# A hybrid decoder trunk on one core: index queries cut to 192 columns, and a list scheduler with new costs and rules

## The chip, the cores and the metric

One core of one Trainium2 chip runs the whole program. The metric is the device time of one execution in microseconds (us). The engines are TensorE (PE in the profile, its weight loads PEld), VectorE (DVE), ScalarE (ACT), GpSimd (POOL) and the queue that issues transfers (SP).

## What is computed

Two layers over 256 tokens of width 2048. In each layer a normed x goes through one large input projection, whose columns feed three branches (a chunked state-space scan, A; a delta-rule recurrence, B; sparse attention with a token indexer, C) and their merge gates; then a branch projection, gated sum, output projection, norm and residual. The part that the change touches directly is the indexer of branch C:

```python
top_k = min(TOPK_MAX, S // 4)                 # 64 of 256 keys
logits_idx = jnp.einsum('bqhd,bsd->bqhs', iqb, ik)
score = jnp.einsum('bqh,bqhs->bqs', iwb, jax.nn.relu(logits_idx))
score = jnp.where(causal[None], score, -jnp.inf)
_, sel = lax.top_k(score, top_k)
valid = sel <= qpos[None, :, None]
```

A query at position below 64 has at most 64 causal keys, so it gets all of them whatever its scores are.

## The kernel before

All projections are products of 128x128 weight blocks with 256 tokens, in float32r with each operand split in a high and a low part: `acc` issues three matmuls for one product of blocks (high by high, high by low, low by high). `block` (L702) runs one block of 128 output columns over the 16 row blocks of the input, so 48 matmuls of 256 columns; `unit` (L713) runs two such blocks into one PSUM tile of the tag `psg` (3 banks). The halves of the weights come by DMA as `wraw`, ScalarE rounds them to `whi`, VectorE subtracts to make `wlo`. The normed input is `hh` (high) and `hl` (low).

`proj_c` (L1264) has the units of branch C: keys, values, then four units of index queries (two heads in each block; 128 columns of weights by 256 tokens), then queries and gates. After each index unit `rope` (L793) makes `iq` from PSUM with four elementwise operations of 128x512: a product on VectorE, a shuffle on VectorE, a product and a sum on GpSimd. `index_scores` (L1186) then makes the scores of each head and `select` (L1207) the mask.

The work of the branches beside the projections uses plain float32 matmuls into PSUM tiles of the tag `psa` (5 banks). A float32 product appears in the trace as two passes, so as two MATMUL records. Most have 128 rows and 128 columns of weights. In `rwkv_chunk` (L1097) there are products of 64x64 weights by 64 columns: the step `pA` has four of them (`UT` with `X`, tile names `ut` and `t`), in a group of two heads whose `X[0]` and two whose `X[1]` was made by another operation; it runs four times for each of eight groups of four heads in the two layers together, 32 times. The step `pB` (`NM` with `SA`, names `b_nm` and `zp`) also has four and runs 16 times.

The order of the instructions on each engine is not that of the program text. `note` (L255) records every operation with its dependencies, its rank (lower goes first) and its cost in ns by the table in `cost` (L289); `issue` (L315) then plays the whole kernel through in a list schedule: when an engine is free at the model's time t it takes, of the recorded operations with all predecessors scheduled, the first by rank and program order whose operands are ready by the model and whose tile has a buffer. A result counts as ready after the operation's end plus a latency: `LP` 200 ns for TensorE, `LD` 140 for VectorE and ScalarE, `PO` 300 for GpSimd, and `LT` 130 more where TensorE is the reader. The order found is what the engines run; on the chip each engine goes through its list in order and waits where an operand is late. The lines of `cost` that the prediction speaks of:

```python
if r[0].dtype in (F32R, BF):
    return n / 2.4 + 1.7, 0.0
if op == "transpose":
    return n / 1.2, 0.0
return n / 0.6 * (0.4 if ... else 0.58 if out.shape[0] <= 64 else 1.05), 0.0
```

Every instruction carries the line of the scheduler's last loop, L418, so groups in the profile are told apart by tile names.

Of the kernel before, what the change touches and what calls it, by code (L numbers as in the profile page):

```python
# [11 lines left out]
F32R = mybir.dt.float32r  # L12
BF = mybir.dt.bfloat16
# [6 lines left out]
DM, S, NL = 2048, 256, 2  # L20
NK = DM // 128
OA, OB, OC, OG = 0, 3088, 7312, 10976
NEG = -1.0e30
GONE = -3.0e38
KAP = 0.5 * math.exp(-0.5)
N1, N2 = 43, 9
WB = 4
# [4 lines left out]
PG = 3  # L32
# [158 lines left out]
    return {"x": x, "post": post, "pos": pos, "par": par, "w2a2": w2a2, "wst": wst, "cst": consts()}  # L191


LP = 200
LD = 140
LT = 130
PT = 180
PO = 300
LW = 0.83
SQ = [(9,), (1, 3)]  # L200

# [1 line left out]
class Program:  # L203
# [51 lines left out]
    def note(self, eng, op, f, a, k):  # L255
        w = [k["out"] if "out" in k else a[0]] + [k[n] for n in ("accum_out",) if n in k]
        r = [x for x in list(a[("out" not in k):]) + [v for n, v in k.items() if n not in ("out", "accum_out")]
             if isinstance(x, bass.AP)]
        i = len(self.ops)
        deps = set()  # L260
        tiles = set()
        for aps, writes in ((r, False), (w, True)):
            for ap in aps:
                g = self.region(ap)
                if g[0] in self.tiles:
                    tiles.add(g[0])
                elif ap.space == bass.MemoryType.DRAM and not g[0].startswith(("diag", "out")):
                    continue
                ws, rs = self.seen.setdefault(g[0], ({}, {}))
                hit = lambda q: q[0] < g[2] and g[1] < q[1] and q[2] < g[4] and g[3] < q[3]  # L270
                deps.update(j for q, j in ws.items() if hit(q))
                if writes or ap.space == bass.MemoryType.PSUM:

                    deps.update(j for j, q in rs.items() if hit(q) and (writes or self.ops[j][0] != eng))
                    inside = lambda q: g[1] <= q[0] and q[1] <= g[2] and g[3] <= q[2] and q[3] <= g[4]
                    for q in [q for q in ws if inside(q)]:
                        del ws[q]
                    for j in [j for j, q in rs.items() if inside(q)]:
                        del rs[j]
                    ws[g[1:]] = i  # L280
                else:
                    rs[i] = g[1:]
        deps.discard(i)
        for t in tiles:
            self.tiles[t][2] += 1
        self.ops.append((eng, op, f, a, k, deps, tiles, self.rank, self.cost(eng, op, w[0], r, k), w[0].shape[0]))

    @staticmethod
    def cost(eng, op, out, r, k):  # L289

        n = int(np.prod(out.shape[1:]))
        if op == "dma_start":
            b = 4.0 * n * out.shape[0]
            return {"SP": 500.0, "ACT": 500.0, "POOL": 1050.0}[eng], b
        if eng == "PE":
            if r[0].dtype in (F32R, BF):
                return n / 2.4 + 1.7, 0.0
            if op == "transpose":
                return n / 1.2, 0.0
            return n / 0.6 * (0.4 if r[0].shape[0] <= 32 or out.shape[0] <= 32 else 0.58 if out.shape[0] <= 64 else 1.05), 0.0  # L300
        m = max([n] + [int(np.prod(x.shape[1:])) for x in r])
        ps = any(x.space == bass.MemoryType.PSUM for x in r)
        sc = sum(int(np.prod(x.shape[1:])) == 1 for x in r) if m > 1 else 0
        if eng == "ACT":
            return (51.0 if ps else 94.0) + 0.833 * m + 93.0 * min(sc, 2) + (46.0 if "accum_out" in k else 0.0), 0.0
        if eng == "DVE":
            fast = op in ("tensor_scalar", "tensor_copy") and not ps
            return 70.0 + (0.52 if fast else 1.042) * m + 61.0 * (sc > 0), 0.0
        if op in ("memset", "affine_select"):
            return 35.0 + (0.83 if op == "memset" else 1.27) * m, 0.0  # L310
        if op == "tensor_scalar":
            return 374.0 * m / 256 + 83.0 * sc, 0.0
        return PT + 2.1 * m, 0.0

    def issue(self, tc):  # L315
        ops = self.ops
# [3 lines left out]
        ready = [0.0] * N  # L320
# [3 lines left out]
                users[j].append(i)  # L324
        cand = {e: [] for e in self.ENGINES}
        add = lambda i: insort(cand[ops[i][0]], (ops[i][7], i))
        for i in range(N):
            if not left[i]:
                add(i)
# [4 lines left out]
        names = {tag: names for tag, (_, names) in self.tags.items()}  # L334
        used = {tag: 0 for tag in self.tags}
        clk = {e: 0.0 for e in self.ENGINES}
        dma = 0.0
        table = 0
        last = 200.0
# [6 lines left out]
        while len(order) < N:  # L346
            t, k, e = heappop(events)
            best = None
            later = None
            until = None  # L350
            for c in cand[e]:
                i = c[1]
                if i > front + AHEAD or until and t + ops[i][8][0] > until:
                    continue
                if ready[i] > t:
                    if c[0] < 0 and ready[i] < t + 250.0 and not until:
                        until = ready[i]
                    later = ready[i] if later is None else min(later, ready[i])
                    continue
                ok = True  # L360
                for n in ops[i][6]:
                    if first[n]:
                        tag, no = self.tiles[n][:2]
                        al, dd = alive[tag], dead[tag]
                        while dd and dd[0][0] <= t:
                            al.remove(heappop(dd)[1])
                        held = used[tag] - (len(names[tag]) - len(al))
                        room = self.tags[tag][0]
                        if held >= room or held >= room - KEEP.get(tag, room) and bisect_left(al, no) >= room:
                            ok = False  # L370
                            break
                if ok:
                    best = c
                    break
# [5 lines left out]
            idle = 0  # L380
            cand[e].remove(best)
            i = best[1]
            _, op, f, a, kw, deps, tiles, _, (busy, b), _ = ops[i]
            order.append(i)
            while front < N and end[front] is not None:
                front += 1
# [1 line left out]
                table = self.TABLES[a[2]]  # L388
                busy += 1300.0
            if e == "PE":  # L390
                w = ops[i][9]
                busy += max(0.0, LW * w - last)
                last = ops[i][8][0]
            clk[e] = t + busy
            if op == "dma_start":
                dma = max(dma, t + busy + 650.0) + b / 360.0
# [3 lines left out]
            for n in tiles:  # L400
                used[self.tiles[n][0]] += first[n]
                first[n] = False
                q = self.tiles[n]
# [4 lines left out]
            for j in users[i]:  # L408
                left[j] -= 1
                to = ops[j][0]  # L410
                ready[j] = max(ready[j], t + busy if to == e == "PE" else end[i] + (LT if to == "PE" else 0.0))
                if not left[j]:
                    add(j)
            heappush(events, (clk[e], k, e))
# [24 lines left out]
class Trunk:  # L439
# [259 lines left out]
        self.mm(out, w[0], x[1], False, False)  # L699
        self.mm(out, w[1], x[0], False, last)  # L700

    def block(self, l, out, x, nch):  # L702

        n = 8 * nch
        for k in range(n):
            if k % 4 == 0:
                w = self.half()
            self.acc(out, [None if q is None else q[:, 128 * (k % 4):128 * (k % 4) + 128] for q in w],
                     [None if q is None else q[k] if isinstance(q, list) else q[:, k, :] for q in x], k == 0, k == n - 1)
            if k % 4 == 3:  # L710
                self.pump()

    def unit(self, l, x, n=2, nch=2):  # L713
        p = self.P("g", PG).rearrange("p (b t) -> p b t", b=2)
        for i in range(n):
            self.block(l, p[:, i, :], x, nch)
        return p

    def split(self, src, hi, lo, scale=None):
# [70 lines left out]
    SWAP = [(i + 16) % 32 for i in range(32)]  # L790

    @urgent
    def rope(self, outs, x, n):  # L793

        P = x.shape[0]
        bc = lambda a: a[:P].to_broadcast([P, n, S])
        t = self.t2(2, S)[:P, :n]
        u = self.t2(2, S)[:P, :n]
        self.v.tensor_tensor(t, x, bc(self.cos), op=OP.mult)
        self.v.stream_shuffle(u, x, self.SWAP)  # L800
        self.g.tensor_tensor(u, u, bc(self.sin), op=OP.mult)
        for o in outs:
            self.g.tensor_tensor(o, t, u, op=OP.add)
# [403 lines left out]
    def select(self):  # L1207
# [6 lines left out]
        for sl in (slice(128, 384), slice(0, 128)):  # L1214
            for _ in range(8):
                yield
                v.max(m8, sc[:, sl])
                v.match_replace(sc[:, sl], m8, sc[:, sl], GONE)
        v.tensor_scalar(sc, sc, 0.9 * GONE, NEG, op0=OP.is_gt, op1=OP.mult)
        kb = self.T([128, 384], "c_kb", 1, BF)  # L1220
# [43 lines left out]
    def proj_c(self, l, h):  # L1264
        s = self.s
        p = self.unit(l, h)
# [8 lines left out]
        for k in range(16):  # L1275
            if k % 2 == 0:
                w = self.half()
# [8 lines left out]
        self.score = self.t2(384)  # L1286
        self.kb = None
        for n in range(4):
            p = self.unit(l, h)
            iq = self.t2(2, S)  # L1290
            self.rope([iq], p, 2)
            self.spawn("C", self.index_scores(iq, n))
            yield
        self.spawn("C", self.select())
        self.yc = self.T([128, 8, S], "yc")
        for n in range(4):
            p = self.unit(l, h)
            if n == 0:
                self.q = self.T([128, 8, S], "ya")
            q = self.q[:, 2 * n:2 * n + 2, :]  # L1300
            self.rope([q], p, 2)
            yield
            p = self.unit(l, h)
# [262 lines left out]
```

## Time and profile before

| | |
|---|---|
| median of 3 runs | 2396.93 us (2394.79 to 2397.88) |
| the profiled execution | 2396.85 us |
| its span, first to last instruction | 2395.1 us |
| PE busy | 2357.6 us, 98% |
| DVE, ACT, POOL busy | 1645.2, 1302.5, 514.3 us |
| mean granted TensorE clock | 0.994 of full speed |

The span and the 1.75 us around it make the execution's own time. A matmul's bar in the trace is longer than its share of the engine, since matmuls are pipelined; what a matmul costs is the distance from its start to the next start.

### The profile page before, as it was taken

The numbers are of one execution on the slowest core, as the hardware profiler recorded it, in microseconds if no ns is written. First come the engines' busy times: TensorE is split into PE (matmuls) and PEld (weight loads), VectorE is DVE, ScalarE is ACT, GpSimd is POOL, SyncE is SP. The second block draws the span as 40 slices with busy tenths as digits, with TensorE's granted clock in tenths as the row PEclk, the third lists the DMA queues.
The fourth block names the chain that finished last, engine by engine and source line by source line (L and its number), as shares of the span: only waits on it lengthen the run. The fifth ranks groups of instructions, "written<-read, shape, count | busy, mean of one in ns | idle before, by whom it ended". The sixth has DMA issues, their size and how long they took to land.

```text
span 2395.1 us, 49317 instructions
## 1 busy us (share of the span) xinstructions
PE 2357.6 (98%) x18750; PEld 2277.0 (95%) x18750; DVE 1645.2 (69%) x3466; ACT 1302.5 (54%) x2674; POOL 514.3 (21%) x915
## 2 busy tenths in 40 slices
PE   8999999999999999999989999999999999999998
PEld 7999999999999999998889999999999999999987
DVE  8865967778795555556576769676787855555565
ACT  5755565656554554445456555656555545545453
POOL 2252252414110000101112513433150100101001
PEclk9999999999999999999999999999999999999999
DMA  5444443535445665656544534434354556656563
GB/s 194 145 159 126 147 152 104 160 108 170 153 150 187 205 225 191 203 187 216 174 143 145 165 118 147 140 119 147 110 188 137 166 186 215 217 187 199 188 214 129
DMA packets 149583, 396.09 MB, mean 165 GB/s; under 512 B 47905, under 2 KB 51937, under 8 KB 149089
## 3 DMA queue, kind: packets, MB, share of 16 engines
q1 hardware_dynamic: 149344, 392.94, 50.4%
q8 instruction: 147, 2.41, 0.4%
q14 instruction: 92, 0.75, 0.1%
HBM read 386.55 MB, written 6.32 MB: 164 GB/s over the span
## 4 chain that ended last, share of the span: by engine, by line
PE 93%; DVE 4%; issue 1%; ACT 1%; DMA 1%; SPq 0%; DVEq 0%; ACTq 0%
PE psg L418 78%; PE psa L418 15%; DVE t L418 2%; DVE wlo L418 1%; DVE yb L418 0%; ACT t L418 0%; DVE ya L418 0%; DMA wraw<-in_wst 0%; DVE n_x L418 0%; ACT whi L418 0%; DMA vd<-diag 0%; DMA yb<-in_x 0%; DVE c_mx L418 0%; SPq L418 0%; DVE yc L418 0%
## 5 line engine op out<-in xcount | busy, mean ns | idle before, releaser
L418 DVE TENSOR_TENSOR wlo<-wraw,whi 128x512 fp32r<-128x512 f32 x1352 | 978.1, 725 | 620.2 <-ACT whi L418 612.9
L418 ACT ACTIVATE whi<-wraw 128x512 fp32r<-128x512 f32 x1361 | 858.2, 632 | 895.9 <-PE psg L418 811.0
L418 PE MATMUL psg<-hh,whi 128*128 128x256 f32 x4224 | 1210.2, 287 | 0.0
L418 PE MATMUL psg<-hl,whi 128*128 128x256 f32 x4224 | 1194.9, 283 | 1.0 <-DVE hl L418 1.0
L418 PE MATMUL psg<-hh,wlo 128*128 128x256 f32 x4224 | 1193.7, 283 | 0.0
L418 PEld LDWEIGHTS psg<-hl,whi 128*128 128x128 f32 x4224 | 796.7, 189 | 6.2 <-DVE hl L418 1.3
L418 PEld LDWEIGHTS psg<-hh,whi 128*128 128x128 f32 x4224 | 796.7, 189 | 5.6 <-issue 1.2
L418 PEld LDWEIGHTS psg<-hh,wlo 128*128 128x128 f32 x4224 | 796.2, 188 | 3.2
L418 PE MATMUL psg<-t,whi 128*128 128x256 f32 x1536 | 274.1, 280 | 0.0
L418 PEld LDWEIGHTS psg<-t,whi 128*128 128x128 f32 x1536 | 234.1, 188 | 0.2
L418 PE MATMUL psg<-t,wlo 128*128 128x256 f32 x768 | 214.8, 280 | 0.0
L418 POOL TENSOR_TENSOR t<-t,t 128x256 f32<-128x256 f32 (+25 forms) x298 | 157.0, 528 | 261.5 <-DVE t L418 179.4
L418 POOL TENSOR_TENSOR b_nm<-b_nm,t 128x256 f32<-128x256 f32 x64 | 47.9, 748 | 737.8 <-DVE t L418 714.8
L418 PEld LDWEIGHTS psg<-t,wlo 128*128 128x128 f32 x768 | 144.3, 188 | 0.1
L418 POOL TENSOR_TENSOR t<-t,d 128x60 f32<-128x60 f32 (+24 forms) x248 | 104.4, 421 | 83.0 <-DMA d<-diag 43.8
L418 ACT ACTIVATE t<-psa 128x256 f32<-128x256 f32 (+5 forms) x230 | 93.4, 426 | 45.4 <-PE psa L418 44.4
L418 PE MATMUL psg<-whi,hh 128*128 128x512 f32 (+1 forms) x268 | 98.8, 369 | 0.0
L418 PE MATMUL psg<-wlo,hh 128*128 128x512 f32 (+1 forms) x268 | 97.8, 365 | 0.0
L418 PE MATMUL psg<-whi,hl 128*128 128x512 f32 (+1 forms) x268 | 97.0, 364 | 0.0
L418 PE MATMUL psa<-t,zp 128*128 128x128 f32 (+1 forms) x448 | 82.5, 299 | 1.1 <-ACT t L418 0.7
L418 PE MATMUL psa<-t,zl 128*128 128x256 f32 x256 | 67.5, 385 | 3.3 <-DVE t L418 2.3
L418 PEld LDWEIGHTS psa<-t,zp 128*128 128x128 f32 x448 | 65.9, 191 | 4.3 <-ACT t L418 1.1
(244 smaller groups left out, 2369.1 us busy)
## 6 DMA issues: line engine op xcount, KB each, us to landing
wraw<-in_wst SPq DMA_DIRECT2D x688, 512.0 KB, 3.4
d<-diag SPq DMA_DIRECT2D x32, 128.0 KB, 3.9
t<-diag SPq DMA_DIRECT2D x16, 256.0 KB, 3.9
d<-in_wst SPq DMA_DIRECT2D x8, 512.0 KB, 5.2
ya<-in_x SPq DMA_DIRECT2D x8, 256.0 KB, 4.3
yb<-in_x SPq DMA_DIRECT2D x8, 256.0 KB, 5.2
b_nm<-in_post SPq DMA_DIRECT2D x2, 1024.0 KB, 6.9
out_x<-ya SPq DMA_DIRECT2D x8, 256.0 KB, 2.8
```

Of the source, the lines that this page charges most:

```text
L418: ops[i][2](*ops[i][3], **ops[i][4])
```

## The change

It cuts the index queries to tokens 64 to 255 and writes zeros for the rest; it replaces costs and one latency of the scheduler; it adds to the model a charge for a change of matmul form and for VectorE and GpSimd running at the same time; and it holds the first matmul of each group of consecutive `psa` matmuls that write one bank. The core of the diff:

```diff
+TOP = 64
+SLACK = 300
+SWITCH = 90
-PT = 180
-PO = 300
+PO = 200
@@ note
+        form = None
+        size = lambda x: int(np.prod(x.shape[1:]))
+        sb = [x for x in r if x.space != bass.MemoryType.PSUM and size(x) > 1]
+        if eng == "PE":
+            cut = lambda n: 32 if n <= 32 else 64 if n <= 64 else 128
+            form = cut(r[0].shape[0]), cut(size(r[0]))
+        elif eng == "DVE":
+            form = size(w[0]) >= 8 and (len(sb) > 1 or len(sb) == len([x for x in r if size(x) > 1])
+                                        and op in ("tensor_scalar", "tensor_copy"))
+        elif eng == "POOL":
+            form = op != "memset"
@@ cost
-                return n / 2.4 + 1.7, 0.0
+                return n * 0.442 + 5.0 if r[0].shape[0] > 64 else n / 1.2, 0.0
             if op == "transpose":
-                return n / 1.2, 0.0
-            return n / 0.6 * (0.4 if ... else 0.58 if out.shape[0] <= 64 else 1.05), 0.0
+                return 30.0, 0.0
+            return 2 * max(n / 1.2 + 2.0, LW * int(np.prod(r[0].shape[1:]))), 0.0
...
-        return PT + 2.1 * m, 0.0
+        return (170.0 if m > 200 else 110.0) + 2.05 * m, 0.0
@@ issue
+        batch = {}
+        run = None
+        for i, o in enumerate(ops):
+            bank = o[0] == "PE" and o[3][0].tensor.name
+            if bank and bank.startswith("psa"):
+                if run is None or run[3] != bank or i - 1 not in batch:
+                    run = [i, 0, 0.0, bank]
+                batch[i] = run
+                run[1] += sum(batch.get(j) is not run for j in o[5])
...
+                late = ready[i]
+                if e == "PE" and i in batch:
+                    if i == batch[i][0]:
+                        if ops[i][10] != (128, 128):
+                            if batch[i][1]:
+                                continue
+                            late = batch[i][2]
+                        if c[0] > 0:
+                            late += SLACK
+                if late > t:
...
             if e == "PE":
-                w = ops[i][9]
-                busy += max(0.0, LW * w - last)
-                last = ops[i][8][0]
+                busy += SWITCH if form != cut else max(0.0, LW * ops[i][9] - last)
+                cut = form
+                last = ops[i][8][0] / (1 if ops[i][3][1].dtype in (F32R, BF) or op == "transpose" else 2)
+            elif form:
+                busy += max(0.0, port["POOL" if e == "DVE" else "DVE"] - t - 55.0)
+                port[e] = t + busy
@@ proj_c, with the slice ts passed on through unit, block and rope
-            p = self.unit(l, h)
+            ts = slice(TOP, S)
+            p = self.unit(l, h, ts=ts)
             iq = self.t2(2, S)
-            self.rope([iq], p, 2)
+            self.g.memset(iq[:, :, 0:TOP], 0.0)
+            self.rope([iq[:, :, ts]], p, 2, ts)
```

`batch[i][1]` counts the operands of the group that are not yet scheduled, `batch[i][2]` is the model's time when the last of them is ready. For a group whose weights are not of the form 128x128 the first matmul is held until all operands of the group are there; for every group of rank over 0 it is held `SLACK` ns longer. ScalarE's costs are also changed by some tens of ns.

## Rows read from the trace of the kernel before

**Rows 1.** The page: busy us and share of the span, instructions.

```profile
PE 2357.6 (98%) x18750; PEld 2277.0 (95%) x18750; DVE 1645.2 (69%) x3466; ACT 1302.5 (54%) x2674; POOL 514.3 (21%) x915
```

**Rows 2.** The page: the chain that ended last, by engine.

```profile
PE 93%; DVE 4%; issue 1%; ACT 1%; DMA 1%; SPq 0%; DVEq 0%; ACTq 0%
```

**Rows 3.** Stretches: us, busy (instructions) of PE, PEld, DVE, ACT, POOL; granted clock, DMA.

```profile
500.00:600.00 100.00, 98.58 (x798) 96.36 (x798) 86.68 (x213) 61.25 (x138) 36.75 (x74) 1.00 0.49 160
...
700.00:1100.00 400.00, 400.00 (x3428) 399.89 (x3428) 232.01 (x372) 202.05 (x352) 27.39 (x42) 1.00 0.60 197
```

**Rows 4.** Timeline of PE around one run of eight 64x64 passes: start us, bar us.

```profile
365.14 0.28 PE L418 MATMUL psg<-hh,whi 128*128 128x256 f32 x1
365.35 0.68 PE L418 MATMUL psa<-zp,b_nm 64*64 64x64 f32 x8
365.95 0.39 PE L418 MATMUL psg<-hl,whi 128*128 128x256 f32 x1
366.18 0.28 PE L418 MATMUL psg<-hh,wlo 128*128 128x256 f32 x1
```

**Rows 5.** Timeline of PE around one run of four 64x64 passes.

```profile
634.05 0.28 PE L418 MATMUL psg<-hh,wlo 128*128 128x256 f32 x1
634.25 0.44 PE L418 MATMUL psa<-t,ut 64*64 64x64 f32 x4
634.63 0.38 PE L418 MATMUL psg<-hh,whi 128*128 128x256 f32 x1
634.85 0.28 PE L418 MATMUL psg<-hl,whi 128*128 128x256 f32 x1
```

**Rows 6.** Groups of PE by form, whole span: count, busy us, mean ns.

```profile
L418 PE MATMUL psa<-t,ut 64*64 64x64 f32 x256 | 28.2, 230 | 0.0
...
L418 PE MATMUL psa<-zp,b_nm 64*64 64x64 f32 x128 | 10.8, 224 | 0.0
```

**Rows 7.** Timeline of PE in the output projection, 512 columns.

```profile
1118.97 0.40 PE L418 MATMUL psg<-whi,hl 128*128 128x512 f32 x1
...
1120.13 0.40 PE L418 MATMUL psg<-wlo,hh 128*128 128x512 f32 x1
```

**Rows 8.** Timeline of PE's weight loads right after a transpose, and in a row of eight.

```profile
300.08 0.19 PEld L418 LDWEIGHTS psg<-hh,whi 128*128 128x128 f32 x1
300.19 0.19 PEld L418 LDWEIGHTS psg<-hl,whi 128*128 128x128 f32 x1
...
211.29 0.86 PEld L418 LDWEIGHTS psa<-cst,vd 128*128 128x128 f32 x8
```

**Rows 9.** A product of `rope` on POOL (whole span) and a small zeroing there.

```profile
L418 POOL TENSOR_TENSOR t<-t,sin 128x512 f32<-128x512 f32 x18 | 29.5, 1636 | 114.9 <-DVE t L418 114.9
...
L418 POOL MEMSET b_cu<- 128x2 f32 x2 | 0.2, 102 | 0.0
```

**Rows 10.** PE's waits, 100 to 1100 us (last: 1260 to 2300): total us, times, longest.

```profile
PE psa L418 <- DVE t L418: 4.3, 7, 1.2
PE psa L418 <- ACT t L418: 0.7, 2, 0.3
PE psa L418 <- POOL t L418: 0.5, 1, 0.5
PE psa L418 <- ACT zl L418: 0.5, 1, 0.5
...
PE psa L418 <- DVE t L418: 4.2, 7, 1.2
```

**Rows 11.** Timeline of PE around one such wait.

```profile
596.13 0.28 PE L418 MATMUL psg<-hh,whi 128*128 128x256 f32 x1
597.30 0.33 PE L418 MATMUL psa<-cst,t 128*128 128x128 f32 x1 [0.90 <-DVE t L418]
```

**Rows 12.** POOL products of 128x256 from 100 to 700 us; VectorE's weight split there.

```profile
L418 POOL TENSOR_TENSOR t<-t,t 128x256 f32<-128x256 f32 x14 | 12.2, 868 | 57.2 <-DVE t L418 38.1 <-DVE c_sm L418 18.0 <-ACT t L418 0.9
...
L418 DVE TENSOR_TENSOR wlo<-wraw,whi 128x512 fp32r<-128x512 f32 x297 | 216.2, 729 | 106.6 <-ACT whi L418 104.3 <-issue 0.5 <-PE psg L418 0.2
```

More of the change, by code (lines that the diff above doesn't have):

```diff
@@ L285, in note @@
             self.tiles[t][2] += 1
-        self.ops.append((eng, op, f, a, k, deps, tiles, self.rank, self.cost(eng, op, w[0], r, k), w[0].shape[0]))
+        form = None
[9 more added lines that the diff above has]
+            form = op != "memset"
+        self.ops.append((eng, op, f, a, k, deps, tiles, self.rank, self.cost(eng, op, w[0], r, k), w[0].shape[0], form))
     @staticmethod
@@ L296, in cost @@
             if r[0].dtype in (F32R, BF):
-                return n / 2.4 + 1.7, 0.0
+                return n * 0.442 + 5.0 if r[0].shape[0] > 64 else n / 1.2, 0.0
             if op == "transpose":
-                return n / 1.2, 0.0
-            return n / 0.6 * (0.4 if r[0].shape[0] <= 32 or out.shape[0] <= 32 else 0.58 if out.shape[0] <= 64 else 1.05), 0.0
+                return 30.0, 0.0
+            return 2 * max(n / 1.2 + 2.0, LW * int(np.prod(r[0].shape[1:]))), 0.0
         m = max([n] + [int(np.prod(x.shape[1:])) for x in r])
@@ L304, in cost @@
         if eng == "ACT":
-            return (51.0 if ps else 94.0) + 0.833 * m + 93.0 * min(sc, 2) + (46.0 if "accum_out" in k else 0.0), 0.0
+            return (51.0 if ps else 105.0) + 0.836 * m + 93.0 * min(sc, 2) + (95.0 if "accum_out" in k else 0.0), 0.0
         if eng == "DVE":
@@ L309, in cost @@
         if op in ("memset", "affine_select"):
-            return 35.0 + (0.83 if op == "memset" else 1.27) * m, 0.0
+            return 35.0 + (0.83 if op == "memset" else 1.32) * m, 0.0
         if op == "tensor_scalar":
             return 374.0 * m / 256 + 83.0 * sc, 0.0
-        return PT + 2.1 * m, 0.0
+        return (170.0 if m > 200 else 110.0) + 2.05 * m, 0.0
     def issue(self, tc):
@@ L336, in issue @@
         clk = {e: 0.0 for e in self.ENGINES}
+        port = {"DVE": 0.0, "POOL": 0.0}
+        cut = None
         dma = 0.0
@@ L354, in issue @@
                     continue
-                if ready[i] > t:
+                late = ready[i]
[8 more added lines that the diff above has]
+                if late > t:
                     if c[0] < 0 and ready[i] < t + 250.0 and not until:
                         until = ready[i]
-                    later = ready[i] if later is None else min(later, ready[i])
+                    later = late if later is None else min(later, late)
                     continue
@@ L382, in issue @@
             i = best[1]
-            _, op, f, a, kw, deps, tiles, _, (busy, b), _ = ops[i]
+            _, op, f, a, kw, deps, tiles, _, (busy, b), _, form = ops[i]
             order.append(i)
@@ L411, in issue @@
                 ready[j] = max(ready[j], t + busy if to == e == "PE" else end[i] + (LT if to == "PE" else 0.0))
+                if j in batch and batch.get(i) is not batch[j]:
+                    batch[j][1] -= 1
+                    batch[j][2] = max(batch[j][2], ready[j])
                 if not left[j]:
@@ L700, in acc, with block @@
         self.mm(out, w[1], x[0], False, last)
-    def block(self, l, out, x, nch):
+    def block(self, l, out, x, nch, ts=slice(0, S)):
         n = 8 * nch
@@ L708, in block, with unit @@
             self.acc(out, [None if q is None else q[:, 128 * (k % 4):128 * (k % 4) + 128] for q in w],
-                     [None if q is None else q[k] if isinstance(q, list) else q[:, k, :] for q in x], k == 0, k == n - 1)
+                     [None if q is None else q[k] if isinstance(q, list) else q[:, k, ts] for q in x], k == 0, k == n - 1)
             if k % 4 == 3:
                 self.pump()
-    def unit(self, l, x, n=2, nch=2):
-        p = self.P("g", PG).rearrange("p (b t) -> p b t", b=2)
+    def unit(self, l, x, n=2, nch=2, ts=slice(0, S)):
+        p = self.P("g", PG).rearrange("p (b t) -> p b t", b=2)[:, :, ts]
         for i in range(n):
-            self.block(l, p[:, i, :], x, nch)
+            self.block(l, p[:, i, :], x, nch, ts)
         return p
@@ L792, in rope @@
     @urgent
-    def rope(self, outs, x, n):
+    def rope(self, outs, x, n, ts=slice(0, S)):
         P = x.shape[0]
-        bc = lambda a: a[:P].to_broadcast([P, n, S])
-        t = self.t2(2, S)[:P, :n]
-        u = self.t2(2, S)[:P, :n]
+        bc = lambda a: a[:P, :, ts].to_broadcast([P, n, ts.stop - ts.start])
+        t = self.t2(2, S)[:P, :n, ts]
+        u = self.t2(2, S)[:P, :n, ts]
         self.v.tensor_tensor(t, x, bc(self.cos), op=OP.mult)
```

## The prediction

> **What bounds the kernel now.** I read the page first: TensorE is busy for 2357.6 of 2395.1 us [rows 1], and the chain of waits that ended last runs 93% through it [rows 2]. A gain has to be time of TensorE. What VectorE, ScalarE or GpSimd save counts only where TensorE waits for them. Busy time is the wrong measure inside TensorE, because bars overlap; the next view is therefore the table of stretches. From 700 to 1100 us only projections run: 3428 matmuls in 400 us, 117 ns each, and no loss [rows 3]. That is the pace of a stream. The granted clock is 1.00 of 2.4 GHz there, and also in the mixed stretch from 500 to 600 us, so the clock is not the question. In that mixed stretch, branch work is put between the projections, and TensorE shows 98.58 of 100 us [rows 3]. The timeline says what is lost: changes of form around 64x64 products [rows 4, 5], and waits for an operand [rows 10, 11]. Both are set by the scheduler.
>
> **Part one, the products by fours.** In [rows 5] a run of four 64x64 passes (two products) stands between projection matmuls. From the projection matmul before the run to the second one after it are 634.85 - 634.05 = 0.80 us; in it stand four passes and two projection matmuls. In [rows 4] the same distance with eight passes is 366.18 - 365.14 = 1.04 us. So four further passes cost 0.24 us, 0.06 each, and the run of four without its passes and without its two matmuls (0.234 us) still costs 0.80 - 0.24 - 0.23 = 0.33 us. That is the price of one interruption: the array goes into the other form and back, and the bars after it start late.
>
> How many interruptions go? [Rows 6] have 256 passes of `ut` and 128 of `b_nm`. By the code each group of four products has eight passes: 32 groups of `pA` and 16 of `pB`. The timeline has every `pB` as one run of eight, as in [rows 4], and every `pA` as two runs of four, as in [rows 5]: 64 runs for 32 groups. The new rule holds the first product until the operands of all four are there; the four follow each other in program order, so TensorE takes them in one go. 32 runs go: 32 x 0.33 = **10.7 us**. What it adds is a wait of the first pair for the second pair's `X`. Behind it on TensorE nothing is queued, because it is held in the model, not on the chip: projection matmuls are put in front. The recurrence gets longer by this and by 0.3 us of `SLACK` in each step, but it must end only before merge `b`, after 12 units of branch A and 16 blocks of merge `c`. The branch work of layer one is over by 700 us, and 400 us of pure projections follow [rows 3]. That covers it; without that cover some 20 steps of about 0.5 us for each group of four heads would be paid.
>
> **Part two, the index queries.** 4 units x 2 blocks x 48 matmuls x 2 layers = 768 matmuls go from 256 columns to 192. Their number stays, and so does each weight load. If the stream alone counted, the price per column comes from two sizes: [rows 7] have five steps of 512 columns in 1120.13 - 1118.97 = 1.16 us, 232 ns each, against 117 for 256: 0.45 ns per column, 29 ns for 64. That would be 22 us in all. But a load of 128 columns of weights must fit beside each matmul, and the trace shows how fast loads follow each other when no long matmul holds them: 300.19 - 300.08 = 0.11 us in float32r, and a row of eight loads for transposes takes 0.86 us, 0.11 each [rows 8]. So 192 columns, some 88 ns by the stream, would stand at the load's 110. The bounds are 0 (nothing below 117 is shown for this shape) and 22 us; I take 110 ns, the row nearest in type and weights: 768 x 7 = **5.4 us**.
>
> The Trainium skill, "TensorE: Matmul & The Clock Gate", section "LDWEIGHTS (loading the stationary operand)", says that a weight load lasts the columns of the weights divided by 1.2 GHz, so 107 ns for 128. By that rule the term would be 768 x 10 = 7.7 us, an estimate from that page; the rule speaks against most of what the cut of columns could bring, and the loads at 0.11 us in [rows 8] agree with it.
>
> The rest of this part lies beside TensorE: eight `rope` calls have operations a quarter shorter, on GpSimd 1636 ns before [rows 9], against eight zeroings of 128 elements. The nearest zeroing took 102 ns for 2 elements [rows 9]; a quarter of 1636 saved covers more than that. GpSimd is at 21% [rows 1], and a product needs its queries only after the rope. I cost this at 0. The products of the scores keep their size.
>
> **Part three, the waits.** The list of waits has 11 for TensorE in layer one, 6.0 us of idle time; layer two repeats it, 7 of them at 4.2 us for VectorE [rows 10]. Idle time starts at a bar's end; the loss is larger: in [rows 11] 597.30 - 596.13 = 1.17 us less one step of 0.117 is 1.05, with 0.90 shown as idle. With 0.15 more for each, 22 waits are about 16 us. All are at the first matmul of a `psa` group. `SLACK` puts each 0.3 us later, which at most gives 22 x 0.3 = 6.6 us. Against it: the old model charged 108.4 ns for a matmul that takes 117, so on the chip every chain on VectorE had 8% more cover than modelled. The new one charges 118.2 and takes that away: 0.25 us for a chain of 3 us. The new charge for VectorE beside GpSimd gives some back. GpSimd's 128x256 product took 868 ns against 718 in the old table, and `wlo` 729 against 603 [rows 12]: both were charged too little, so part of the waits have their cause there. Bounds: -16 us (all waits go) and +16 (as many more); I take **-4 us**, over half of what `SLACK` can give.
>
> The start of the program and the seam between the layers hold no index unit and no `pA`; their order may shift by a microsecond or two either way, and I put 0.
>
> **The sum.** -10.7 - 5.4 - 4 = -20.1 us on the profiled execution's 2396.85 us (span 2395.1 and 1.75 around it), which is within 0.1 of the median, 2396.93: **2376.8 us**. Own range of this case: fours 8 to 11, index 0 to 8, waits -12 to +4, so 2366 to 2391.
>
> **Rivals.** *Columns count in full.* If the next load starts early enough, the 768 matmuls go at the stream's pace, 29 ns less each: 22 instead of 5.4 us, so 2360 us. For it: at 256 and 512 columns the time goes with the columns [rows 3, 7]. Against it: loads never stand closer than 0.11 us [rows 8]. Chance 0.11.
>
> The skill has a rule for this too: the same page, section "Back-to-back issue gap", gives columns / 2.4 + 2.5 ns for isolated matmuls, so 26.7 ns less for 64 columns, an estimate of 20.5 us in all. At 256 columns it would give 109 ns, and the trace has 117.
>
> *The fours do not form.* Another branch matmul, earlier in program order, may become ready after the first product and be put between, as projections are now. Then the 32 runs stay and 2396.85 - 9.4 = 2387 us is left. For it: the rule holds only the first matmul of a group. Against: the next three have neighbouring program places, and the window is 0.3 us. Chance 0.10.
>
> *The honest costs bring more waits, and it gets slower.* TensorE's list is fixed, so a modelled time that is too early is paid in full at the first matmul of a `psa` group. The place is the stretch from 500 to 600 us, where VectorE is busiest, 86.68 of 100 us [rows 3]. The change takes 8% of cover and 0.1 us of GpSimd's latency (`PO`), while `wlo` stays charged 0.13 us too low [rows 12]. A wait there loses about 0.7 us (16 us by 22). Gains of 16 us from parts one and two are lost when 23 more waits appear, and 0.2% slower needs some 30 more, 52 in all, on the several hundred groups: 2402 us and over, 2405 as its middle. For it: the waits now stand behind VectorE [rows 10]. Against it: 0.3 us of `SLACK` on every group is more than each of these losses. Chance 0.08.
>
> **How the numbers follow.** Forecast 0.71 (some 0.04 of it between 2392 and 2398), columns 0.11, no fours 0.10 (some 0.03 above 2392), slower 0.08. About 0.2% (4.8 us) is what a measurement of this kernel can tell from no change. Faster by over 0.2%: 0.85; within: 0.07; slower: 0.08. The range runs from 2358, to hold the columns' case, to 2392; outside it lie the slower case, 0.07 within 0.2%, and little below.
>
> **What the profile after would show.** Fours: `ut` passes in runs of eight only, distances of 1.04 us as in [rows 4]; 48 runs where there were 80. Index: 768 matmuls of 192 columns, steps of 110 ns if the load bounds them, 88 if the stream does, 117 if nothing is won. Waits: fewer than 22 lines for `psa`, shorter than 1.2 us; if they are more, the third rival holds. The stretches without branch work must stay at 117 ns a matmul; if they do not, something else than these parts has changed. The prediction is wrong if the time is over 2392 with the fours formed, or if a new wait of TensorE on `psg` appears, for `whi` or `wlo`.

## The result and the profile after

The changed kernel takes 2356.68 us (median, 2356.22 to 2357.03) against 2395.98 us for the kernel before in the same runs: a ratio of 0.9835, 95% interval 0.9818 to 0.9852. That is 39 us less, where 20 were forecast, and 1.3 us outside the range, whose low end was 2358. The profiled execution has a span of 2355.3 us, 39.8 less than before.

The page of the changed kernel, engines and chain:

```profile
PE 2331.2 (99%) x18750; PEld 2261.7 (96%) x18750; DVE 1626.8 (69%) x3466; ACT 1298.9 (55%) x2672; POOL 522.7 (22%) x923
...
PE 96%; DVE 2%; DMA 1%; ACT 1%; POOL 0%; issue 0%; SPq 0%; POOLq 0%; ACTq 0%; DVEq 0%
```

TensorE issues as many matmuls as in [rows 1] in 40 us less, and the share of VectorE in the chain fell from 4% [rows 2] to 2%. Something that TensorE waited for has gone.

Its timeline of PE around a `pA` group, to set beside [rows 4, 5]:

```profile
213.29 0.28 PE L460 MATMUL psg<-hh,whi 128*128 128x256 f32 x1
213.50 0.67 PE L460 MATMUL psa<-t,ut 64*64 64x64 f32 x8
214.11 0.38 PE L460 MATMUL psg<-hl,whi 128*128 128x256 f32 x1
214.33 0.28 PE L460 MATMUL psg<-hh,wlo 128*128 128x256 f32 x1
```

`ut` now stands in runs of eight, and the distance is 214.33 - 213.29 = 1.04 us, as forecast. The timeline has 48 runs of `pA` and `pB` passes in all, each of eight, where before had 80.

Its timeline of PE in an index unit:

```profile
114.90 0.25 PE L460 MATMUL psg<-hh,whi 128*128 128x192 f32 x1
114.99 0.27 PE L460 MATMUL psg<-hl,whi 128*128 128x192 f32 x1
115.10 0.27 PE L460 MATMUL psg<-hh,wlo 128*128 128x192 f32 x1
...
115.55 0.27 PE L460 MATMUL psg<-hh,whi 128*128 128x192 f32 x1
115.65 0.27 PE L460 MATMUL psg<-hl,whi 128*128 128x192 f32 x1
```

From 114.99 to 115.65 are six steps, 110 ns each: the step of the weight load in [rows 8], not the 88 ns of the columns. The median of all such steps in this trace is 113 ns, against 117 at 256 columns.

PE's waits, first from 100 to 1100 us, then from 1240 to 2280 us:

```profile
PE psa L460 <- DMA ut<-diag: 0.4, 1, 0.4
PE psa L460 <- POOL t L460: 0.2, 1, 0.2
PE psa L460 <- DVE sbd L460: 0.2, 1, 0.2
...
PE psa L460 <- POOL t L460: 0.2, 1, 0.2
PE psa L460 <- DVE sbd L460: 0.2, 1, 0.2
```

Here is the surprise. [Rows 10] had 11 waits and 6.0 us of idle time for layer one alone; 5 waits and 1.2 us are left for both layers. The branch stretch of layer one in the table of stretches, kernel before and then after:

```profile
100.00:700.00 600.00, 593.96 (x4779) 573.19 (x4777) 453.97 (x1076) 340.13 (x761) 193.55 (x377) 1.00 0.45 142
```

```profile
100.00:700.00 600.00, 599.15 (x4916) 583.09 (x4915) 461.61 (x1108) 347.03 (x771) 195.64 (x380) 1.00 0.46 147
```

In the same 600 us TensorE gets through 137 matmuls more. At 600 / 4779 = 0.126 us each this is 17 us. All these kernels take the `psg` matmuls in the same order, so the start of the same one marks equal work (us from the span's start; the last column is a run described below, the kernel before with a hold of 1200 ns):

| `psg` matmul | before | changed | hold 1200 |
|---|---|---|---|
| the 301st, early in layer one | 59.1 | 60.0 | 58.5 |
| the 7578th, after layer one's branch work | 1105.1 | 1086.7 | 1088.2 |
| the 8601st, early in layer two | 1301.5 | 1279.4 | 1280.7 |
| the 15542nd, after layer two's branch work | 2295.1 | 2255.4 | 2258.8 |

Between the first two marks 19.3 us went, between the last two 17.6, and 3.7 in the seam between the layers. Of the 36.9 us in the two layers the fours are 32 x 0.33 = 10.7 and the index queries 3.7 (below). Some 22 us are left, where I had put 4 for the waits. The waits that the list names are about 15 of them: between the marks it has 24 lines and 14.3 us of idle time before, 6 lines and 1.9 us after, and each line loses about 0.16 us more than its idle time. Where the other 7 us went is not shown.

### The profile page after: what moved, and what is told of

Same layout as the page of the kernel before. It is cut to its first block, busy times and chain, and to the rows that moved or that the text cites. A ratio compares the mean times of both kernels' runs of the same rounds, so it can differ in the third digit from the quotient of the medians.

```text
span 2355.3 us, 49352 instructions
## 1 busy us (share of the span) xinstructions
PE 2331.2 (99%) x18750; PEld 2261.7 (96%) x18750; DVE 1626.8 (69%) x3466; ACT 1298.9 (55%) x2672; POOL 522.7 (22%) x923
## 4 chain that ended last, share of the span: by engine, by line
PE 96%; DVE 2%; DMA 1%; ACT 1%; POOL 0%; issue 0%; SPq 0%; POOLq 0%; ACTq 0%; DVEq 0%
PE psg L460 81%; PE psa L460 15%; DVE t L460 1%; DVE n_x L460 0%; ACT t L460 0%; DMA yb<-in_x 0%; DVE yb L460 0%; POOL t L460 0%; DVE wlo L460 0%; DMA t<-diag 0%; SPq L460 0%; DMA ut<-diag 0%; ACT whi L460 0%; DVE whi L460 0%; DVE sbd L460 0%
## 5 line engine op out<-in xcount | busy, mean ns | idle before, releaser
L460 PE MATMUL psg<-hh,whi 128*128 128x256 f32 (+1 forms) x4224 | 1205.9, 285 | 0.0
L460 PE MATMUL psg<-hh,wlo 128*128 128x256 f32 (+1 forms) x4224 | 1190.4, 282 | 0.0
L460 PE MATMUL psg<-hl,whi 128*128 128x256 f32 (+1 forms) x4224 | 1189.7, 282 | 0.0
L460 POOL TENSOR_TENSOR t<-t,t 128x256 f32<-128x256 f32 (+24 forms) x298 | 158.4, 533 | 235.3 <-DVE t L460 193.7
L460 DVE SCALAR_TENSOR_TENSOR t<-t,t 128x256 f32<-128x256 f32 (+1 forms) x158 | 69.3, 443 | 0.8 <-ACT t L460 0.4
```

The lines of the kernel that those rows point to most:

```text
L460: ops[i][2](*ops[i][3], **ops[i][4])
```

## The experiments

Each run changes the kernel before or the changed kernel in one or a few of the parts; ratios are to the kernel before, run beside it on the same chip, with 95% intervals.

| what | median us | ratio |
|---|---|---|
| changed, index at 256 columns | 2360.43 | 0.9853 [0.9839, 0.9868] |
| changed, index at 128 columns (leaves out the scores of tokens 64 to 127) | 2355.42 | 0.9833 [0.9818, 0.9848] |
| changed, no rule for the fours | 2358.94 | 0.9848 [0.9831, 0.9864] |
| changed, hold 0 | 2362.43 | 0.9858 [0.9842, 0.9875] |
| changed, no charge for VectorE beside GpSimd | 2407.14 | 1.0050 [1.0035, 1.0065] |
| changed, TensorE's old costs, no charge for a change of form | 2350.06 | 0.9810 [0.9795, 0.9825] |
| the same, hold 600 | 2349.94 | 0.9809 [0.9794, 0.9823] |
| before, charge alone | 2367.68 | 0.9884 [0.9869, 0.9899] |
| before, hold 300 alone | 2386.60 | 0.9963 [0.9950, 0.9976] |
| before, hold 1200 alone | 2359.73 | 0.9851 [0.9836, 0.9865] |
| before, mean durations alone | 2372.49 | 0.9902 [0.9888, 0.9917] |
| before, TensorE's new costs alone | 2419.02 | 1.0099 [1.0082, 1.0116] |
| changed, no charge, hold 1200 | 2398.26 | 1.0009 [1.0000, 1.0018] |
| the same, old costs and latency but TensorE's | 2376.44 | 0.9917 [0.9900, 0.9934] |
| before, index, fours, hold 1200 | 2356.92 | 0.9841 [0.9824, 0.9857] |
| before, index, fours, charge, hold 600 | 2352.13 | 0.9819 [0.9804, 0.9833] |

Two of these ratios are clearly apart from about 0.0023 on, which is 5 us (two half-widths of 0.0016, added in squares). The effects below of 2 to 4 us are smaller than this and rest on what the traces show beside them.

**The index queries.** First at 256 columns again:

```diff
-            ts = slice(TOP, S)
-            p = self.unit(l, h, ts=ts)
+            p = self.unit(l, h)
-            self.g.memset(iq[:, :, 0:TOP], 0.0)
-            self.rope([iq[:, :, ts]], p, 2, ts)
+            self.rope([iq], p, 2)
```

> The changed kernel with the index queries back at 256 columns, all else kept. Theory load (a 192-column matmul stands at its weight load's 0.11 us): 768 x 5 to 7 ns come back, 2361 to 2363 us. Rival columns (time goes with the columns, 29 ns each): 2379 us. In the trace of the changed kernel the 192-column steps are 113 ns in the median, so I expect the first, with 3 to 5 us.

2360.43 us: the cut is worth 3.7 us, as 768 steps 5 ns shorter. The medians of the steps, 117 and 113 ns, would give 3.1. Then at 128 columns:

```diff
-TOP = 64
+TOP = 128
```

> The changed kernel with the index queries cut to tokens 128 to 255, so it leaves out the scores of tokens 64 to 127, which then get keys by order. The 768 matmuls have 128 columns. Theory load (weight loads set the step): still 109 to 113 ns, 2354 to 2357 us. Rival columns: 0.45 ns a column, 29 ns less each, 2334 us.

2355.42 us, 1.3 us less than with 192, which the intervals do not tell apart. The timeline of PE in this kernel, the same place:

```profile
114.95 0.27 PE L460 MATMUL psg<-hh,wlo 128*128 128x128 f32 x1
...
115.62 0.27 PE L460 MATMUL psg<-hh,wlo 128*128 128x128 f32 x1
```

These two stand six steps apart, 0.67 us or 112 ns each, with two thirds of the columns. Columns no longer set the step, and it stands where the weight loads of [rows 8] follow each other; the rival that columns count in full has fallen.

**The fours.** The rule that holds the first product is taken out:

```diff
-                        if ops[i][10] != (128, 128):
-                            if batch[i][1]:
-                                continue
-                            late = batch[i][2]
```

> The changed kernel without the rule that holds a 64x64 group until all its operands are there. My step of 32 interruptions at 0.33 us: 2356.7 + 10.7 = 2367 us, with 80 runs of 64x64 passes in the trace again. If the honest costs and the charge for a change of form already keep the products together: 2357 to 2360 us.

2358.94 us, 2.3 us slower. Its timeline shows the split that is back in some places:

```profile
211.36 0.44 PE L456 MATMUL psa<-t,ut 64*64 64x64 f32 x4
211.73 0.39 PE L456 MATMUL psg<-hh,whi 128*128 128x256 f32 x1
212.05 0.44 PE L456 MATMUL psa<-t,ut 64*64 64x64 f32 x4
```

It is back in 12 places, not in 32: 60 runs against 48. At 0.33 us these are 4.0 us, of which 2.3 showed. The other 20 groups stay whole without the rule; by the code this means that the second pair was ready, in the model, when the first was taken. The hold has a part in that: with it alone, in the kernel before, the timeline has 70 runs at 300 ns and 52 at 1200.

**The hold.**

```diff
-SLACK = 300
+SLACK = 0
```

> The changed kernel with SLACK 0. Theory slack (the 0.3 us hold is what removed TensorE's waits in the mixed stretches, 17 us): most come back, 2366 to 2374 us, and the waits list shows some 20 lines again. Rival costs (the honest costs and the charge for VectorE beside GpSimd removed them): within 3 us of the changed kernel, 2357 to 2360.

2362.43 us, 5.7 us slower. Neither theory had it: the hold is worth something, but the waits of [rows 10] don't come back with it gone. What its list shows instead is another wait, for a transfer, in layer two:

```profile
PE psa L460 <- DMA vd<-diag: 3.7, 2, 2.0
```

The changed kernel has no such line, so some 4 us of what this run lost are these two waits.

**The charge for VectorE beside GpSimd.** It is taken out of the changed kernel:

```diff
-            elif form:
-                busy += max(0.0, port["POOL" if e == "DVE" else "DVE"] - t - 55.0)
-                port[e] = t + busy
```

> The changed kernel without the charge for VectorE and GpSimd running together. Theory slack: 2357 to 2360 us. Rival costs: the waits behind VectorE come back, since the model believes VectorE too early, 2362 to 2372 us.

2407.14 us: 50 us slower, and slower than the kernel before. PE's waits from 100 to 700 us:

```profile
PE psa L456 <- POOL t L456: 7.7, 4, 3.4
PE psa L456 <- DVE t L456: 5.1, 7, 1.3
```

I had expected 2372 us at most. So my third rival was real, and in the changed kernel the hold of 300 ns did not keep it away; the charge did. The same lines alone, put into the kernel before:

> The kernel before with one thing added: the model's charge for VectorE and GpSimd running together. Theory port (that charge is what removed TensorE's waits, 17 us in the mixed stretches of before): 2375 to 2385 us against 2395.5, and the waits list of the mixed stretches nearly empty. Rival interplay (the charge only repairs what the honest TensorE costs broke, 50 us in the run without it): 2392 to 2398 us.

2367.68 us, 27 us faster, more than the 10 to 20 that I expected. One wait is left from 100 to 1100 us where [rows 10] had 11:

```profile
PE psa L456 <- DVE t L456: 0.4, 1, 0.4
```

It keeps nearly all interruptions (78 runs of the `pA` and `pB` passes), so little of the 27 us is interruptions; I take it for waits.

**TensorE's costs.** The old table in the changed kernel:

```diff
-                return n * 0.442 + 5.0 if r[0].shape[0] > 64 else n / 1.2, 0.0
+                return n / 2.4 + 1.7, 0.0
...
-                busy += SWITCH if form != cut else max(0.0, LW * ops[i][9] - last)
+                busy += max(0.0, LW * ops[i][9] - last)
...
-                last = ops[i][8][0] / (1 if ops[i][3][1].dtype in (F32R, BF) or op == "transpose" else 2)
+                last = ops[i][8][0]
```

> The changed kernel with TensorE's old cost table and without the charge of 90 ns for a change of form. The old table charges a projection matmul 8% too little, which gave chains on other engines cover. By the step of the prediction that the honest costs take cover away: equal or some us faster, 2350 to 2357 us. Rival costs (a model in pace with the chip puts the first matmul of a group where its operand really is): slower, 2360 to 2370.

2350.06 us, 6.6 us faster than with the honest costs (those that follow the measured steps). Then the new table and the charge for a change of form alone in the kernel before:

> The kernel before with one thing added: TensorE's new costs and the 90 ns for a change of form. Theory cover (the old costs, 8% low, give the other engines cover that the honest ones take away; without the charge for VectorE beside GpSimd nothing replaces it): slower, 2400 to 2412 us, with more than 22 waits in the mixed stretches. Rival (honest costs alone help): 2380 to 2393 us.

2419.02 us, 23 us slower, more than the 16 that I expected at most, with VectorE's waits from 100 to 700 us (4.3 us before, [rows 10]) at

```profile
PE psa L452 <- DVE t L452: 7.2, 8, 3.1
```

A model nearer to the chip made a slower kernel. The list explains only a part: between the marks of the table above its idle time grows by 5 us, from 14.3 to 19.6. Short waits grow by 7 more, from 3 to 10 us; by these I mean steps without a line, over 30 ns longer than usual, that end with a late operand. The seam takes 2 more, and the rest is not placed.

**Cover or knowledge?** The charge might work because the model then knows which operations are late, or because anything that makes results late in the model keeps TensorE's list safe. The hold alone in the kernel before, with `SLACK` at 300 and at 1200:

```diff
+                        if c[0] > 0:
+                            late += SLACK
```

> The kernel before with one thing added: the hold of 300 ns on the first matmul of each group. Theory port: the old model is wrong by more than 0.3 us where GpSimd runs, so a part of 4 to 7 us, as much as the hold was worth in the changed kernel (5.7 us): 2389 to 2392 us. Rival slack (0.3 us on each of 22 waits): the same at most 6.6 us; so this run sizes the term and doesn't tell them apart.

2386.60 us, 8.5 us faster, a little more than the 4 to 7 expected.

> The kernel before with the hold on the first matmul of each group at 1200 ns, and nothing else. Theory any cover (TensorE's waits, the longest 1.2 us, go with any hold of their length): 2368 to 2378 us, as with the charge for GpSimd alone (2367.7). Theory place (only knowing which operations are late puts the work right, since one late operation delays the chain behind it in the model too): 2380 to 2390 us.

2359.73 us: 36.5 us from one constant, more than the charge and more than either theory had. It has 28 interruptions fewer (52 runs), 9 us by their price; that leaves some 27. Then the mean durations instead of the charge:

```diff
-            return 70.0 + (0.52 if fast else 1.042) * m + 61.0 * (sc > 0), 0.0
+            two = sum(x.space != bass.MemoryType.PSUM and int(np.prod(x.shape[1:])) > 1 for x in r) > 1
+            return 70.0 + (0.52 if fast else 1.28 if two else 1.042) * m + 61.0 * (sc > 0), 0.0
...
-        return PT + 2.1 * m, 0.0
+        return 1.2 * (180.0 + 2.1 * m), 0.0
```

> The kernel before with VectorE's operations of two SBUF inputs charged 1.28 ns an element instead of 1.042 and GpSimd's products 1.2 times as much, the mean durations of the trace, and no charge for running together. Rival mean (the table was too low on average): 2368 to 2378 us. Theory exclusion (single operations are held until the other engine ends, up to 1.2 us, which a mean does not show): less than half of the 27 us, 2383 to 2396 us.

2372.49 us, 24 of the charge's 27. My theory that only the charge can place single late operations has fallen: under the old costs an average does nearly as well. Under the new costs the hold had its limit:

> The changed kernel without the charge for VectorE and GpSimd running together (2407.1 us), and with the hold on the first matmul of a group at 1200 instead of 300 ns. Theory cover (the charge acts as cover in the model, and a longer hold does the same): 2355 to 2365 us. Rival knowledge (with honest TensorE costs the model has to know which operations are late): over 2375 us.

2398.26 us, 9 us less than with the hold at 300; the rival holds here. PE's waits from 100 to 1100 us:

```profile
PE psa L456 <- POOL t L456: 7.9, 6, 2.4
PE psa L456 <- DVE t L456: 2.6, 5, 0.8
```

They are up to 2.4 us long, on top of a hold of 1.2. One more run puts back GpSimd's latency of 300 ns and the old costs of all engines but TensorE:

> The changed kernel without the charge for running together, with the hold at 1200 ns (2398.3 us), and with the old latency of GpSimd (300 ns) and the old costs of all engines but TensorE. Theory pool (what the hold could not cover is GpSimd's own lateness, which its lower latency and costs made, 16.7 us of waits behind it): those waits fall under 4 us and the time to 2365 to 2380 us. Rival pace (TensorE's honest pace leaves every chain without cover): over 2388 us.

2376.44 us: 22 us of the loss are these costs and this latency, and `POOL t` falls to

```profile
PE psa L456 <- POOL t L456: 1.4, 2, 0.8
```

What still parts this kernel from the next one is TensorE's costs alone, 2376.44 against 2356.92, 19.5 us.

**The parts that are enough.** The kernel before with the index cut, the fours and a hold of 1200, and no new cost:

> The kernel before with the index queries cut, the rule of the fours, and the hold at 1200 ns; old costs, old latencies, no charge. Theory cover: the parts add, 2359.7 - 3.7 for the index columns - 4 interruptions in each layer at 0.33 us, so 2353 to 2356 us, at least as fast as the whole change (2356.7). Rival: over 2359 us.

2356.92 us, just over the 2353 to 2356 expected, and level with the whole change (the intervals overlap). With the charge and a hold of 600:

> The kernel before with the index cut, the fours, the charge for VectorE beside GpSimd and the hold at 600 ns; no other new cost or latency. If the shorter latency of GpSimd and the small cost changes are worth nothing: 2347 to 2351 us, as the changed kernel with TensorE's old costs (2350).

2352.13 us, also just over what I expected. And the changed kernel with TensorE's old costs and a hold of 600:

> The changed kernel with TensorE's old costs (2350.1 us) and the hold at 600 instead of 300 ns. Some 12 waits of 0.1 us each are left in the mixed stretches: 2348 to 2351 us. If longer chains now come late behind the projections: 2351 to 2356 us.

2349.94 us, as with 300 (2350.06). In the branch stretches the list has one wait of 0.2 us left. These two runs with TensorE's old costs beat both kernels, by 6.7 us under the changed one.

## Why the prediction was wrong

**Part one held in its price and its count.** A run of eight takes 1.04 us again, as the price of 0.33 us has it, and 32 of 80 interruptions went. What was wrong is whose work it is: without the rule only 12 come back, with 2.3 us; the other changes of the model keep the rest together.

**Part two held.** 3.7 us against 5.4, with the step near where [rows 8] put it: 113 ns in the median at 192 columns and 112 at 128. The rival that columns count in full had a chance of 0.11, and nothing speaks for it. The rule of the Trainium skill, "TensorE: Matmul & The Clock Gate", section "LDWEIGHTS (loading the stationary operand)", of 107 ns for 128 columns agrees within 6 ns.

**Part three failed.** I took -4 us for the waits, and some 22 went in the two layers, at least 15 of them waits of the list. The sentence "The new charge for VectorE beside GpSimd gives some back" is the step: I set its worth below the loss of cover from TensorE's costs and took -4 us for all together. By itself the charge is worth 27 us in the kernel before and 50 us in the changed one. What I had argued against it was right in its sign: TensorE's honest costs alone lose 23 us in the kernel before, and 6.6 in the changed one. The balance of two large terms was taken for a small one.

The bound of -16 us fits the waits that the list names: about 15 us of them went. It is too narrow for all that went, since a list has no line for a wait shorter than what the bar hides (0.28 us of bar less 0.117 of step). With the hold of 1200 ns alone, 31.8 us went in the two layers by the table of equal work; less 9 for interruptions some 22 are left there too. Short waits are a part of what goes beyond the list, but only 3 us of them stand in the trace of before; what the rest is stays open. The seam between the layers, which I had put at 0, gave 3.7 us in the changed kernel and 3.9 with the hold.

The own range of the case was also added up wrongly: its bounds give 2393 us at the upper end and not 2391. Nothing hangs on it.

The evidence for the charge stood in the trace of before, and I read past it, because I looked at a mean: `wlo` took 729 ns with GpSimd busy a third of the time [rows 12] and 725 where it is nearly idle, from 700 to 1100 us, which looks like no contention at all:

```profile
L418 DVE TENSOR_TENSOR wlo<-wraw,whi 128x512 fp32r<-128x512 f32 x284 | 205.7, 725 | 167.1 <-ACT whi L418 166.9
```

The median is 692 ns in both stretches, and the longest are 1807 and 1274 ns. Over the whole span the `wlo` that overlap no GpSimd operation but a zeroing took 659 to 697 ns, and the 319 that do took 838 in the mean. Single operations show why. VectorE and GpSimd of the kernel before, in one place:

```profile
404.76 0.34 DVE L418 TENSOR_SCALAR t<-t,c_sm 128x256 f32<-128x256 f32 x1
405.03 1.24 DVE L418 TENSOR_SCALAR c_mx<-c_mx 128x2 f32<-128x2 f32 x1
406.18 0.68 DVE L418 TENSOR_TENSOR wlo<-wraw,whi 128x512 fp32r<-128x512 f32 x1
...
404.84 1.41 POOL L418 TENSOR_TENSOR ya<-t,t 128x512 f32<-128x512 f32 x1
```

and the durations of that small operation (ns, least, median, most):

```profile
L418 DVE TENSOR_SCALAR c_mx<-c_mx x32: 148/159/1246, 294.6 to 1722.1; 128x2 f32<-128x2 f32 x32
```

It works on two elements in each partition and takes 159 ns in the median. Here it takes 1.24 us, from 405.03 to 406.27, and ends when GpSimd's sum does, 404.84 + 1.41 = 406.25. The other one of this length, in layer two at 1594.35, also ends 0.02 us after the same sum. The old model knew nothing of that: the softmax that waits for `c_mx` runs on ScalarE, and its product stands on TensorE's list too early, as this wait of the same place shows:

```profile
407.72 0.70 PE L418 MATMUL psa<-t,zp 128*128 128x256 f32 x2 [0.34 <-ACT t L418]
```

The Trainium skill, "SBUF — State Buffer", section "SBUF: two separate sides", says that VectorE in some forms and GpSimd hold a shared pair of ports one at a time, for a whole instruction. These rows agree with it.

**The rivals.** The slower one had the mechanism right, and nearly its time: without the charge the changed kernel takes 2407 us, where I had 2405 as the middle of the case. Its chance came out low for a wrong reason, `SLACK`, which is worth 5.7 us; what kept it away was the charge. "The fours do not form" did not come about.

## What to carry to other kernels

Where one engine is full and its order is fixed ahead by a model, the model's error counts on one side only: an operand expected too early stops the full engine, one expected too late costs little while other work can be put in its place. So when a cost in such a model is made honest, look for the cover that the dishonest one gave, and price both; and try one constant of extra lateness first, since here a single hold of 1200 ns alone gave 36 us, nearly as much as the whole change (39). It did so under the old costs; under the honest ones it did not replace the charge (2398 us). A list of waits is a lower bound of what waiting costs, and a mean duration can hide that one engine waits for another; look at the longest instance of a short operation.

## What the runs showed of the hardware

- A change from 128x128 to 64x64 matmuls and back costs 0.33 us beyond the passes themselves: 0.80 us around four passes and 1.04 around eight in [rows 4, 5], and 1.04 around eight in the changed kernel.
- Float32r matmuls of 128 and of 192 columns with 128 columns of weights come at the same pace, 112 and 113 ns in the median; 256 columns come at 117. Fewer columns than some 240 would buy nothing (110 ns / 0.45 ns per column, an estimate from [rows 3, 7, 8]).
- An operation of VectorE on 128x2 elements that began during a GpSimd sum of 128x512 elements took 1.24 us, eight times its median of 159 ns, and ended with the sum; so did its counterpart in layer two.
